# Float32 scores for two attentions, on two halves of TensorE's rows

## The chip, the cores and the metric

The kernel runs on one core of one Trainium2 chip. The metric is the device time of one execution in microseconds (us); lower is better. All data are in float32 outside the chip. TensorE takes its operands either as plain float32 or as float32r, a rounded form that the program makes with a cast.

## The reference

A bidirectional encoder of two layers over 1024 tokens of width 1024. In each layer a mixing block joins three groups of features, and a gated feed-forward block follows:

```python
for l in range(DEPTH):
    h = _rmsnorm(x, g_pre_mix[l])
    zf, zq, zk, zv, zm = jnp.split(h @ w_in[l], splits, axis=-1)
    y_f = _fourier_mix(zf, w_fourier[l])
    q = _rope(zq.reshape(b, s, 8, 64), positions)
    k = _rope(zk.reshape(b, s, 2, 64), positions)
    y_a = _window_attn(q, k, zv.reshape(b, s, 2, 64), sink[l])
    km, vm = jnp.split(_rmsnorm(mem, g_mem[l]) @ w_mem_kv[l], 2, axis=-1)
    y_m = _memory_attn(zm.reshape(b, s, 4, 64), km, vm)   # km, vm: 256 rows, 4 heads
    y = jnp.concatenate([_rmsnorm(y_f, ...), _rmsnorm(y_a, ...), _rmsnorm(y_m, ...)], axis=-1) @ w_out[l]
    x = x + _rmsnorm(y, g_post_mix[l])
    h = _rmsnorm(x, g_pre_ffn[l])
    gate, up = jnp.split(h @ w_ffn_in[l], 2, axis=-1)
    x = x + _rmsnorm((jax.nn.silu(gate) * up) @ w_ffn_out[l], g_post_ffn[l])
```

The window attention has 8 query heads of 64 channels in two groups of four; each group shares one key and value head. A block of 128 queries sees the keys of its own block and of its two neighbours, so 256 keys at the edges and 384 elsewhere, and the softmax has one extra "sink" term for each head. The memory attention has 4 heads of 64 channels over 256 memory rows, and no mask.

## The kernel before

**Precision.** Most products run in float32r. To keep accuracy, an operand is split in two float32r parts: `hi` is a cast by ScalarE (line 176) and `lo` the difference, by VectorE or GpSimd (line 177). A product of split operands is then several float32r matmuls that add up in PSUM (`Acc`, line 187). A few products are plain float32, which TensorE carries out as two instructions each.

**Order of the work.** One instruction stream for each engine; a scheduler orders it from a timeline of its own, with the order of the source as priority, so matmuls of neighbouring streams are interleaved. `weave` mixes lists of units. In each layer the stages run in this order: the Fourier input and the projection of keys, values and memory queries (`kvz`), woven with the Fourier group; the projection of queries (`q`), woven with the memory attention (`mem_units`); the first window group (`att_units(0)`), woven with the output projection of the Fourier and memory groups (`fm_units`, tile `mo`); the second window group (`att_units(1)`) with the output projection of the window group (`out`), the residual and the preparation of the feed-forward blocks (`hb`). The two feed-forward products take the rest of a layer.

**Stacks.** A head has 64 channels, half of the array's 128 rows. The scores use all rows by stacking: `q_stacks` puts the cast of a head's queries on its own 64 partitions and the difference on the other 64, one such tile for each head of a pair (line 435 casts on ScalarE, line 438 subtractions on VectorE). It serves the window queries (`q_turn`, 128 x 512 at a time) and the memory queries (`kvz_turn`, tile `zT`). `dup_stacks` writes the keys likewise, the cast on both halves (lines 424 and 425) and the difference on both halves (428 and 429); it serves the window keys (`kvz_turn`, tile `kT`) and the memory keys (`Memory.load`, from a DMA). The lines 424 to 438 in the profile are these two helpers.

**Scores.** For each head, two float32r matmuls add up in one PSUM bank: the stacked queries against the keys' cast, and against the keys' difference. In the window attention (line 788, tile `sc`) they are 256 or 384 wide and each head has a PSUM tile of its own from the tag `sc` (two tiles). One VectorE instruction adds the mask and takes the maximum (line 789); then ScalarE does the exponential (801) and GpSimd the division (812). In the memory attention (line 901, tile `ms`) a unit is one head with half of the tokens, in two PSUM tiles of 2 x 256 columns; VectorE takes the maxima (903), ScalarE the exponentials with their sums (906), GpSimd the division (912).

**Values.** TensorE transposes the probabilities (825 and 922, tiles `pT` and `mpT`) and they are copied out of PSUM. The first window group splits them (176, 177) and multiplies them by a stack of the values' cast and difference, 512 columns for four heads, twice (840); `fold` then adds the two halves of the result (861 to 863). The second window group copies them unsplit (830) and runs plain float32 (833): heads 0 and 2 on one half of the array's columns, 1 and 3 on the other, 256 columns each; `values_32` adds the values' two parts together beforehand. The memory values are plain float32 in the same manner (932), 512 columns for a head, its two heads from two units.

**Memory.** All SBUF tiles lie in two arenas, one of float32r and one of float32, at hand-chosen places given in units of 1 KB for each partition. A place can be given over to a tile of the other type (`reflex`, `turned`, table `TURNED`). PSUM has 8 banks, shared out by tags (`PS_BUFS`): `sc`, `pT`, `av` and `pd`, two tiles of one bank each.

## Time and profile before

| what | us |
|---|---|
| median of three timed runs | 2032.31 |
| lowest and highest of them | 2031.08, 2033.2 |
| the profiled execution | 2032.38 |
| its span, first to last instruction | 2030.4 |

The granted TensorE clock has a mean of 0.994 of full speed over the span. The feed-forward products fill about 404 to 1000 us in the first layer and 1403 us to the end in the second; the change's stages lie at about 67 to 383 and 1039 to 1380 us.

How to read the profile: PE is TensorE's matmuls, PEld its weight loads, DVE VectorE, ACT ScalarE, POOL GpSimd. `L788` is line 788 of the kernel before. `sc<-arena_r` names the tile written and those read. In `128*128 128x384 f32` the first two numbers are the rows and columns of the array that are in use and the last two the output; `128*64` is a matmul on half of the columns. A group's row has its count, then busy us and mean ns of one, then idle time of the engine before it and what ended it. Matmuls are pipelined and their shown ends are modelled, so the distance from one start to the next says what one costs, not its shown duration. A float32 matmul other than a transpose stands in the profile as two instructions.

### The profile page before, as it was taken

The page shows a single profiled execution, that of the slowest core. Times are in us where ns is not written, and L with a number is a line of the kernel's source. Part 1 is how long each engine was busy: PE and PEld are TensorE (multiplying, and loading weights), DVE is VectorE, ACT ScalarE, POOL GpSimd, SP SyncE. Part 2 cuts the span into 40 slices and gives each one's busy share as a digit, 9 for nine tenths or more (in the row PEclk, how much of TensorE's full clock was granted, in tenths as well). Part 3 has the DMA queues.
Part 4 walks back from the last instruction along what each step waited for, and adds up shares of the span by engine and source line. Part 5 has one row for each costly group of instructions (what it writes and reads, how often), then busy time and mean ns, then how long its engine had stood idle before and what let it go on. Part 6 is the DMA issues. An engine that isn't in the chain of part 4 may idle for free.

```text
span 2030.4 us, 28325 instructions
## 1 busy us (share of the span) xinstructions
PE 1984.7 (98%) x9587; PEld 1631.2 (80%) x9587; DVE 1492.6 (74%) x2346; ACT 1049.7 (52%) x2204; POOL 684.9 (34%) x811
## 2 busy tenths in 40 slices
PE   8999999999999999999999999999999999999998
PEld 7877878778888888887888778877788888887886
DVE  5566767897877776778876668679786776778766
ACT  6476877643333333554555768686333333346441
POOL 4344445224334333002423644451433433410011
PEclk9999999999999999999999999999999999999999
DMA  6110333434333324879831113244333323269973
GB/s 213 62 58 22 109 104 115 146 109 130 104 109 100 103 88 139 297 266 324 286 142 54 54 58 115 85 144 135 106 118 114 116 82 114 96 209 354 314 265 125
DMA packets 181889, 288.56 MB, mean 142 GB/s; under 512 B 15560, under 2 KB 81648, under 8 KB 181744
## 3 DMA queue, kind: packets, MB, share of 16 engines
q1 hardware_dynamic: 173680, 267.88, 39.7%
q10 hardware_dynamic: 8064, 18.88, 2.4%
q8 instruction: 75, 1.23, 0.2%
q14 instruction: 70, 0.57, 0.1%
HBM read 220.11 MB, written 66.58 MB: 141 GB/s over the span
## 4 chain that ended last, share of the span: by engine, by line
PE 86%; DVE 5%; DMA 3%; ACT 2%; issue 2%; POOL 1%; SPq 0%; DVEq 0%; POOLq 0%; ACTq 0%
PE fo L1330 17%; PE qc L1181 11%; PE qx L1181 11%; PE qy L1181 11%; PE mo L187 8%; PE qz L1181 5%; PE kvp L187 4%; PE qp L187 3%; PE zT L187 2%; PE sc L788 2%; PE pT L825 2%; PE av L833 1%; PE qa L1181 1%; PE mav L932 1%; PE av L840 1%
## 5 line engine op out<-in xcount | busy, mean ns | idle before, releaser
L1330 PE MATMUL fo<-arena_r 128*128 128x512 f32 x1512 | 354.2, 391 | 6.0 <-ACT big L1355 3.8
L1330 PEld LDWEIGHTS fo<-arena_r 128*128 128x128 f32 x1512 | 283.6, 188 | 65.6 <-ACT big L1355 4.6
L176 ACT CAST arena_r<-arena_f 128x512 fp32r<-128x512 f32 (+2 forms) x344 | 185.9, 571 | 179.5 <-DMA arena_f<-actd 66.6
L1181 PE MATMUL qc<-arena_r,flex 128*128 128x512 f32 x912 | 220.2, 390 | 0.0
L177 DVE TENSOR_TENSOR arena_r<-arena_f,arena_r 128x512 fp32r<-128x512 f32 x262 | 182.0, 727 | 46.9 <-ACT arena_r L176 39.0
L1171 ACT CAST flex<-arena_f 128x512 fp32r<-128x512 f32 x148 | 91.9, 621 | 235.0 <-PE qy L1181 73.3
L1181 PEld LDWEIGHTS qc<-arena_r,flex 128*128 128x128 f32 x912 | 171.2, 188 | 37.0
L1181 PE MATMUL qy<-arena_r,flex 128*128 128x512 f32 x576 | 139.9, 390 | 2.3 <-ACT flex L1171 2.3
L1171 ACT CAST arena_r<-arena_f 128x512 fp32r<-128x512 f32 x92 | 57.1, 621 | 159.1 <-DVE arena_f L1168 63.6
L1172 DVE TENSOR_TENSOR flex<-arena_f,flex 128x512 fp32r<-128x512 f32 x148 | 110.9, 750 | 28.4 <-ACT flex L1171 28.2
L1181 PEld LDWEIGHTS qy<-arena_r,flex 128*128 128x128 f32 x576 | 107.9, 188 | 25.3 <-ACT flex L1171 2.7
L1215 POOL TENSOR_TENSOR arena_f<-arena_f 128x512 f32<-128x512 f32 x36 | 47.3, 1315 | 237.5 <-ACT arena_f L1186 237.5
L1181 PE MATMUL qx<-arena_r 128*128 128x512 f32 x360 | 119.5, 389 | 0.0
L1181 PE MATMUL qy<-arena_r 128*128 128x512 f32 x480 | 116.7, 390 | 0.0
L1172 DVE TENSOR_TENSOR arena_r<-arena_f,arena_r 128x512 fp32r<-128x512 f32 x92 | 68.2, 742 | 63.2 <-ACT arena_r L1171 62.8
L1181 PE MATMUL qz<-arena_r,flex 128*128 128x512 f32 x320 | 106.8, 395 | 0.0
L1181 PEld LDWEIGHTS qy<-arena_r 128*128 128x128 f32 x480 | 90.3, 188 | 18.9 <-ACT arena_r L1171 0.2
L1168 DVE TENSOR_TENSOR arena_f<-arena_f 128x512 f32<-128x512 f32 x90 | 98.1, 1098 | 5.5 <-DMA arena_f<-in_w_ffn_in 3.9
L1222 POOL TENSOR_TENSOR arena_f<-arena_f 128x512 f32<-128x512 f32 x36 | 60.0, 1667 | 120.2 <-DVE arena_f L1221 120.2
L187 PE MATMUL mo<-big,arena_r 128*128 128x512 f32 x384 | 100.2, 399 | 0.3 <-ACT arena_f L1031 0.2
L1181 PE MATMUL qx<-flex,flex 128*128 128x512 f32 x304 | 100.1, 390 | 0.0
L1242 POOL TENSOR_TENSOR arena_f<-arena_f,flex 128x512 f32<-128x512 f32 x32 | 51.8, 1619 | 139.5 <-ACT flex L1233 83.7
(315 smaller groups left out, 4659.8 us busy)
## 6 DMA issues: line engine op xcount, KB each, us to landing
arena_f<-in_w_ffn_out SPq DMA_DIRECT2D x264, 256.0 KB, 4.7
actd<-arena_f SPq DMA_DIRECT2D x154, 256.0 KB, 2.5
arena_f<-actd SPq DMA_DIRECT2D x154, 256.0 KB, 4.4
arena_f<-in_w_ffn_in SPq DMA_DIRECT2D x46, 512.0 KB, 3.7
big<-in_w_ffn_in SPq DMA_DIRECT2D x40, 512.0 KB, 4.5
arena_f<-in_w_in SPq DMA_DIRECT2D x40, 256.0 KB, 2.9
arena_f<-in_x SPq DMA_DIRECT2D x16, 512.0 KB, 4.3
arena_f<-in_w_out SPq DMA_DIRECT2D x32, 256.0 KB, 2.7
```

The source lines that it names most:

```text
L176: nc.scalar.copy(hi, src)
L177: return (lo_eng or nc.vector).tensor_tensor(out=lo, in0=src, in1=f32(hi), op=ALU.subtract)
L187: mm(self.dst, a, b, start=self.i == 0, stop=self.i == self.n - 1)
L788: mm(pt, lhs, self.kst[g][i][:, k0 * P : k1 * P], start=i == 0, stop=i == 1)
L1168: nc.vector.tensor_tensor(out=s, in0=x, in1=y, op=op)
L1171: self.cast = nc.scalar.copy(w[:, 0], s)
L1172: nc.vector.tensor_tensor(out=w[:, 1], in0=s, in1=f32(w[:, 0]), op=ALU.subtract)
L1181: mm(pt, a, b, start=start and n == 0, stop=n == 11, skip_group_check=not start)
L1215: G(out=self.u2, in0=self.u2, in1=self.p1, op=ALU.add)
L1222: G(out=self.p5, in0=self.p1, in1=self.p5, op=ALU.add)
L1242: (G if i % 2 else V).tensor_tensor(out=a[i], in0=c, in1=g[i], op=ALU.mult)
L1330: mm(pt, ab[:, 0, x, sl], ab[:, 1, y], start=new and first and j == 0, stop=last and j == 2, skip_group_check=not new)
```

## The change

The scores of both attentions become plain float32. Queries, keys and memory queries are copied unsplit; the two heads of a pair lie on partitions 0 to 63 and 64 to 127 and their products are issued one behind the other, each on its 64 rows of the array, into the two banks of one PSUM tile with the new tag `s2` (one tile). A memory unit becomes a pair of heads with a quarter of the tokens. The first window group's values take the second's form, with the evacuating copies in turn on VectorE and ScalarE. `dup_stacks`, `q_stacks`, `fold` and `values_32` go. Places in the arenas move, and some PSUM tags are exchanged.

```diff
-TURNED = {32: 8, 56: 8, 112: 8, 120: 4}
+TURNED = {16: 8, 32: 8, 56: 8, 64: 8, 72: 8, 80: 8, 96: 8, 104: 8, 112: 8, 120: 4}
-PS_BUFS = {"sc": 2, "pT": 2, "av": 2, "pd": 2}
+PS_BUFS = {"sc": 2, "pT": 2, "av": 2, "pd": 2, "s2": 1}
...
         def load(self):
-            raw = at(32, 2, NMEM)
-            nc.sync.dma_start(raw, kvd[self.l, :, 0:512].rearrange("p (i c) -> p i c", i=2))
+            self.k = at(32, 2, NMEM)
+            nc.sync.dma_start(self.k, kvd[self.l, :, 0:512].rearrange("p (i c) -> p i c", i=2))
...
-            km = shaped(reflex(F32R), (2, 2, 2, NMEM))
-            self.km = [km[:, i] for i in range(2)]
-            for ci in range(2):
-                dup_stacks([(self.km[ci][:, j, 0], self.km[ci][:, j, 1]) for j in range(2)], raw[:, ci])
...
             def products(r):
-                pt = ps([256], "yfp", "sc")
+                pt = ps([256], "yfp", "av")
...
         def kvz(self, t):
-            split(vst[:, :, 0, :], vst[:, :, 1, :], r[:, P : 2 * P].rearrange("p (g d) -> p g d", g=2), nc.gpsimd)
+            nc.gpsimd.tensor_copy(self.v32[:, :, t, :], r[:, P : 2 * P].rearrange("p (g d) -> p g d", g=2))
...
         def kvz_turn(self, t):
-            q_stacks([self.zst[half][j][:, :, c * P : c * P + P] for j in range(2)], zt)
+            nc.scalar.copy(self.zf[:, half, :, c * P : c * P + P], zt)
...
-                dup_stacks([(self.kst[g][0][:, sl], self.kst[g][1][:, sl]) for g in range(2)], ktf)
+                for g, copy in enumerate((nc.scalar.copy, nc.vector.tensor_copy)):
+                    for o in range(2):
+                        copy(self.kf[64 * o : 64 * o + 64, g, sl], ktf[64 * g : 64 * g + 64])
...
         def q_turn(self, t):
-            q_stacks([self.qst[half][j][:, :, c * P : c * P + P] for j in range(2)], qt)
+            nc.scalar.copy(self.qf[half][:, :, c * P : c * P + P], qt)
...
         def att_scores(self, g, n):
-            for h in range(4):
-                pt = ps([W], "sc", "sc")
-                lhs = self.qst[half][h % 2][:, 2 * g + h // 2, c * P : c * P + P]
-                for i in range(2):
-                    mm(pt, lhs, self.kst[g][i][:, k0 * P : k1 * P], start=i == 0, stop=i == 1)
-                nc.vector.tensor_tensor_reduce(
...
+            for hp in range(2):
+                pt = ps([2, 512], "sc", "s2")
+                pts = [pt[:, s, :W] for s in range(2)]
+                for s in range(2):
+                    r = slice(64 * s, 64 * s + 64)
+                    mm(pts[s], self.qf[half][r, 2 * g + hp, c * P : c * P + P], self.kf[r, g, k0 * P : k1 * P], start=True, stop=True)
+                for s in range(2):
+                    nc.vector.tensor_tensor_reduce(
...
         def att_values(self, g, n, es_, dst):
-                pp = phs(2, 512, dt=F32R)
-                ph, pl = pp[:, 0], pp[:, 1]
-                split(ph, pl, pT.rearrange("p h q -> p (h q)"))
-                lhs = self.vst[(k0 + j) // 4][:, (k0 + j) % 4, g].rearrange("p a d -> p (a d)")
-                for i, p_ in enumerate((ph, pl)):
-                    mm(av, lhs, p_, start=j == 0 and i == 0, stop=j == nk - 1 and i == 1)
+                pf = self.pfs[self.pfi % 4]
+                self.pfi += 1
+                (nc.vector.tensor_copy if (self.pfi % 2 and not g) else nc.scalar.copy)(pf, pT.rearrange("p (k s) q -> p s k q", s=2))
+                for s in range(2):
+                    rhs = pf[:, s].rearrange("p k q -> p (k q)")
+                    mm(av[64 * s : 64 * s + 64, 0 : 2 * P], self.v32[:, g, k0 + j], rhs, start=j == 0, stop=j == nk - 1)
+            nc.scalar.copy(dst, av[:, 0 : 2 * P].rearrange("p (k q) -> p k q", k=2))
...
+        def mem_scores(self, half, pr, b):
...
+            pt = ps([2, 2, NMEM], "ms", "s2")
+            pts = [pt[:, s] for s in range(2)]
+            for j in range(2):
+                c = 2 * b + j
+                for s in range(2):
+                    r = slice(64 * s, 64 * s + 64)
+                    mm(pts[s][:, j], self.zf[r, half, pr, c * P : c * P + P], self.mem.k[r, pr], start=True, stop=True)
+            for s in range(2):
+                nc.vector.tensor_reduce(out=nmx[:, 2 * s : 2 * s + 2], in_=pts[s], axis=AX.X, op=ALU.max, negate=True)
...
         def mem_turn(self, e):
-                pf = mps(512)
-                nc.scalar.copy(pf, pT.rearrange("p h q -> p (h q)"))
+                pf = mps(2, 256)
+                nc.scalar.copy(pf, pT.rearrange("p s j q -> p s (j q)"))
...
-        def mem_values(self, pr, half, pfs):
-            av = ps([512], "mav", "av")
+        def mem_values(self, half, pr, b, pfs):
+            av = ps([256], "mav", "av")
...
-                    mm(av[64 * s : 64 * s + 64], self.mem.v[:, mt, 2 * pr + s], pfs[s][mt], start=mt == 0, stop=mt == 1)
+                    mm(av[64 * s : 64 * s + 64], self.mem.v[:, mt, 2 * pr + s], pfs[mt][:, s], start=mt == 0, stop=mt == 1)
...
-        HB = {1: (64, 72), 2: (80, 88), 5: (16, 24), 6: (96, None), 3: (0, 8), 7: (32, 40), 4: (104, None)}
+        HB = {1: (64, 104), 2: (80, 72), 5: (16, 24), 6: (96, None), 3: (0, 8), 7: (32, 40), 4: (88, None)}
...
-            pt = ps([512], "qa", "sc")
+            pt = ps([512], "qa", "s2")
...
-                self.c11 = ps([512], "qc", "pT")
+                self.c11 = ps([512], "qc", "sc")
...
-                self.x = ps([512], "qx", "sc")
+                self.x = ps([512], "qx", "pT")
```

More of the change, by code (lines that the diff above doesn't have):

```diff
@@ L716, in kvz @@
             if c == 0:
-                self.vst[half] = at(96 + 4 * half, 4, 2, 2, HD, dt=F32R)
-                z = at(104 + 8 * half, 2, 2, 512, dt=F32R)
-                self.zst[half] = [z[:, i] for i in range(2)]
                 if half == 0:
-                    kst = at(80, 2, 2, S, dt=F32R)
-                    self.kst = [[kst[:, i, j] for j in range(2)] for i in range(2)]
+                    self.v32 = turned(96, 2, 2, NT, HD)[:, 0]
+                    self.zf = turned(104, 2, 2, 512)
+                    self.kf = turned(80, 2, S)
             pt = ps([512], "kvp")
@@ L772, in q_turn @@
             if c == 0:
-                self.qst[half] = [at((64, 0)[half] + 8 * i, 4, 512, dt=F32R) for i in range(2)]
-            q_stacks([self.qst[half][j][:, :, c * P : c * P + P] for j in range(2)], qt)
+                self.qf[half] = turned((64, 72)[half], 4, 512)
+            nc.scalar.copy(self.qf[half][:, :, c * P : c * P + P], qt)
         def att_scores(self, g, n):
@@ L825, in att_values @@
                     nc.tensor.transpose(pT[:, h, :], es_[h // 2][:, h % 2, j * P : j * P + P], ident)
-                if g:
-                    pf = self.pfs[self.pfi % 4]
-                    self.pfi += 1
-                    nc.scalar.copy(pf, pT.rearrange("p (k s) q -> p s k q", s=2))
-                    for s in range(2):
-                        rhs = pf[:, s].rearrange("p k q -> p (k q)")
-                        mm(av[64 * s : 64 * s + 64, 0 : 2 * P], self.v32[:, k0 + j], rhs, start=j == 0, stop=j == nk - 1)
-                    continue
@@ L846, in values_32 @@
-        def values_32(self):
-            self.v32 = at(4, NT, HD)
-            for half in range(2):
-                v = self.vst[half][:, :, 1]
-                nc.gpsimd.tensor_tensor(out=self.v32[:, 4 * half : 4 * half + 4], in0=f32(v[:, :, 0]), in1=f32(v[:, :, 1]), op=ALU.add)
-            pf = turned(112, 4, 2, 2, P)
-            self.pfs, self.pfi = [pf[:, i] for i in range(4)], 0
-        def fold(self, av, dst):
-            cut = lambda ap: ap.rearrange("p (h s q) -> p s h q", s=2, q=P)
-            avh, avl = cut(av[0:64]), cut(av[64:128])
-            d = [dst[64 * s : 64 * s + 64] for s in range(2)]
-            for s in range(2):
-                nc.scalar.copy(d[s], avl[:, s])
-            for s in range(2):
-                nc.vector.tensor_tensor(out=d[s], in0=avh[:, s], in1=d[s], op=ALU.add)
+                pf = self.pfs[self.pfi % 4]
@@ new lines, in att_values, with att_begin @@
+                self.pfi += 1
[4 more added lines that the diff above has]
+            nc.scalar.copy(dst, av[:, 0 : 2 * P].rearrange("p (k q) -> p k q", k=2))
+        def att_begin(self, g):
+            pf = turned((16, 112)[g], 4, 2, 2, P)
+            self.pfs, self.pfi = [pf[:, i] for i in range(4)], 0
+            if g:
+                v = at(4, NT, HD)
+                nc.gpsimd.tensor_copy(v, self.v32[:, 1])
+                self.v32 = v[:, None].to_broadcast([P, 2, NT, HD])
+                reflex(F32R, 16)
+                reflex(F32R, 96)
@@ L910, in mem_scores @@
             nc.vector.reciprocal(rden, den)
-            for b in range(4):
-                nc.gpsimd.tensor_scalar(
-                    out=e[b // 2][:, b % 2], in0=e[b // 2][:, b % 2], scalar1=rden[:, b : b + 1], scalar2=1.0, op0=ALU.mult, op1=ALU.mult
-                )
+            for i in range(4):
+                ei = e[i // 2][:, i % 2]
+                nc.gpsimd.tensor_scalar(out=ei, in0=ei, scalar1=rden[:, i : i + 1], scalar2=1.0, op0=ALU.mult, op1=ALU.mult)
             return e
@@ L942, in unit @@
                     st[i] = self.mem_scores(*todo[i])
[L943 to L945 removed]
+                if i >= 2:
+                    if i == 2:
                         ym = at(24, 2, 2, 512)
                         self.ym = [ym[:, i] for i in range(2)]
[L948 removed]
+                    self.mem_values(*todo[i - 2], pp.pop(i - 2))
                 if 1 <= i <= n:
@@ L1455, in tile_encoder @@
                 uq.load_part(0, at(44, 2, 4, P))
-                reflex(F32R, 112)
+                for k in (72, 80, 112):
+                    reflex(F32R, k)
                 gq.step(1)
```

67 lines of the change are left out of this document (18 added, 49 removed).

## Prediction

> **What bounds the kernel now.** I read the page first, then busy time by stage, the engine's own waits, the groups of matmuls by shape, and last the timeline of TensorE around the places that change. The page, engines and the chain that ended last:
>
> ```profile
> PE 1984.7 (98%) x9587; PEld 1631.2 (80%) x9587; DVE 1492.6 (74%) x2346; ACT 1049.7 (52%) x2204; POOL 684.9 (34%) x811
> ...
> PE 86%; DVE 5%; DMA 3%; ACT 2%; issue 2%; POOL 1%; SPq 0%; DVEq 0%; POOLq 0%; ACTq 0%
> ```
>
> The columns of the next view are stretch, length, then busy us (instructions) of PE, PEld, DVE, ACT and POOL. The stretches of the first layer are those of the memory attention, of the first window group, and of the second.
>
> ```profile
> 138.00:204.00 66.00, 63.90 (x331) 48.99 (x330) 45.50 (x75) 40.80 (x114) 30.32 (x51) 0.97 0.06 19
> 204.00:290.00 86.00, 83.52 (x449) 69.44 (x449) 65.44 (x196) 67.61 (x182) 37.93 (x63) 1.00 0.35 117
> 290.00:383.00 93.00, 91.17 (x531) 72.17 (x530) 64.81 (x134) 66.11 (x164) 45.66 (x77) 0.98 0.36 122
> ```
>
> The reader is to see that TensorE is the bound in each of the three stages (97%, 97% and 98% busy), and that VectorE and ScalarE, which the change relieves, stand at 62 to 79%. Their work counts only where TensorE waited for it. Those waits, of TensorE alone, us in total, times, longest:
>
> ```profile
> PE av L840 <- DVE flex L863: 2.0, 2, 1.3
> ...
> PE qp L187 <- DVE big L407: 1.7, 1, 1.7
> ...
> PE ms L901 <- ACT flex L425: 1.3, 1, 1.3
> ...
> PE ssp L988 <- DVE arena_r L438: 1.1, 2, 0.8
> PE ms L901 <- DVE flex L438: 0.8, 1, 0.8
> ```
>
> These five hang on the splits that go (L425 the keys' casts, L438 subtractions for q, z and keys, L863 the fold) or stand behind them in VectorE's queue (L407, a weight split amid the key splits). Together 6.9 us: nearly all the waiting that the change can take away. So the forecast is a sum over TensorE's work.
>
> **What a matmul costs now.** The groups (line, shape, count | busy us, mean ns; a float32 product shows as two instructions):
>
> ```profile
> L788 PE MATMUL sc<-arena_r 128*128 128x384 f32 x192 | 49.0, 355 | 0.1
> L788 PE MATMUL sc<-arena_r 128*128 128x256 f32 x64 | 12.7, 298 | 0.5 <-ACT arena_f L906 0.3 <-DVE rmax L789 0.2
> L840 PE MATMUL av<-arena_r 128*128 128x512 f32 x88 | 31.0, 420 | 2.2 <-DVE flex L863 2.0 <-DVE arena_r L177 0.2
> L833 PE MATMUL av<-flex,arena_f 128*64 128x256 f32 x176 | 26.3, 398 | 0.0
> L932 PE MATMUL mav<-arena_f 128*64 128x512 f32 x64 | 23.4, 612 | 0.0
> L901 PE MATMUL ms<-flex,arena_r 128*128 128x256 f32 x64 | 10.4, 289 | 2.1 <-ACT flex L425 1.3 <-DVE flex L438 0.8
> L901 PE MATMUL ms<-flex,flex 128*128 128x256 f32 x64 | 10.2, 286 | 0.0
> ```
>
> The mean durations overlap, so they don't add up. What one costs is read from the starts of consecutive timeline rows (start, length, line, shape, count):
>
> ```profile
> 160.05 0.64 PE L901 MATMUL ms<-flex,arena_r 128*128 128x256 f32 x4
> 160.52 0.40 PE L187 MATMUL qp<-big,flex 128*128 128x512 f32 x1
> ...
> 280.86 1.07 PE L840 MATMUL av<-arena_r 128*128 128x512 f32 x4
> 281.77 0.87 PE L788 MATMUL sc<-arena_r 128*128 128x384 f32 x4
> 282.48 0.86 PE L187 MATMUL mo<-big,arena_r 128*128 128x512 f32 x3
> ...
> 293.82 0.65 PE L833 MATMUL av<-flex,arena_f 128*64 128x256 f32 x4
> 294.40 0.61 PE L988 MATMUL ssp<-const,arena_f 128*128 128x2 f32 x4
> ...
> 298.34 0.88 PE L788 MATMUL sc<-arena_r 128*128 128x384 f32 x4
> 299.14 0.65 PE L833 MATMUL av<-flex,arena_f 128*64 128x256 f32 x4
> ...
> 308.07 1.52 PE L833 MATMUL av<-flex,arena_f 128*64 128x256 f32 x12
> 309.52 0.96 PE L187 MATMUL mo<-flex,arena_r 128*128 128x512 f32 x3
> 310.32 0.40 PE L187 MATMUL mo<-arena_r 128*128 128x512 f32 x1
> ```
>
> Split (float32r) products, four each: 160.52 - 160.05 = 0.47 us at 256 columns, 282.48 - 281.77 = 0.71 at 384, 281.77 - 280.86 = 0.91 at 512 (0.23 each). A float32 pair on two halves of the array's columns, 256 wide, is four instructions: 0.58 alone (294.40 - 293.82), and three pairs 1.45 (309.52 - 308.07). So each further pair costs (1.45 - 0.58)/2 = **0.435**, and a run of pairs has 0.145 of its own. The rest of its price falls on its neighbours: four score products ahead of a run took 0.80 (299.14 - 298.34) instead of 0.71, 0.09 more; behind it three 512-wide products took 0.80 (310.32 - 309.52) instead of 3 x 0.23, 0.11 more. A run thus costs 0.145 + 0.09, and up to 0.11 where a split product follows: 0.24 to 0.35 beside its streaming; I take **0.30**, the middle. The streaming itself, 0.435 for two heads at 256 columns, is what split products need too (0.47).
>
> **The change part by part.**
>
> *Window scores.* Per two heads, four split products give way to one float32 pair on two halves of the rows. There are 64 such pairs (192/4 = 48 wide, 64/4 = 16 narrow). No pair on row halves stands in the trace; the nearest row is the pair on column halves. Streaming scales to 0.435 x 1.5 = 0.65 at 384. Wide: 0.65 + 0.30 - 0.71 = +0.24, x48 = 11.5; narrow: 0.435 + 0.30 - 0.47 = +0.265, x16 = 4.2. Together **+15.7**. The bounds are a run that costs nothing extra (64 x 0.30 = 19.2 less) and halves that run one after the other (rival 2).
>
> *Memory scores.* 128 split products in 16 units; a unit's eight took 0.94. Now two pairs in one run: 0.87 + 0.30 = 1.17, so +0.23 x16 = **+3.7**.
>
> That entering a row tile costs anything has one row, a transpose on 8 rows of the array:
>
> ```profile
> 25.64 0.62 PE L187 MATMUL zT<-arena_r 128*128 128x512 f32 x2
> 26.20 0.23 PE L262 MATMUL posT<-const,flex 8*128 8x8 f32 x1
> 26.35 1.20 PE L187 MATMUL zT<-arena_r 128*128 128x512 f32 x4
> ```
>
> The two products ahead took 0.56 instead of 0.46, 0.10 more, as ahead of a column run, and the tiny transpose held the engine 0.15. So I take the column price for rows. The Trainium skill, TensorEngine Tiling (Array Packing), Tiling Modes, Key Properties, says that changing the tiling mode drains TensorE; that speaks against the change, and by it the sum is the forecast's, without it rival 1's. The Trainium skill, TensorE: Matmul & The Clock Gate, Part 3, says that tiles on different rows run together with starts some 4 ns apart; no run here shows it for rows, and by it rival 2 falls away.
>
> *First group's values.* 88 split products of 0.23 (20.3) become 44 pairs of 0.435 (19.1) as in the second group, whose 176 instructions (44 pairs, from 293.82 to 1368.9) came in 33 runs: 19.1 + 33 x 0.30 = 29.0, **+8.7**; bounds 22 and 44 runs, +5.4 and +12.
>
> *Memory values.* Now some heads' products run alone:
>
> ```profile
> 205.06 1.07 PE L932 MATMUL mav<-arena_f 128*64 128x512 f32 x2
> 206.06 0.50 PE L788 MATMUL sc<-arena_r 128*128 128x256 f32 x2
> ```
>
> One product, 1.00 us, with half the columns empty. After, both heads of a pair come from one evacuated tile, so 32 pairs of 256 columns: 32 x 0.435 + 16 to 32 runs x 0.30 = 18.7 to 23.5, against 23.4 busy now. I take **-3**.
>
> *Neighbouring runs.* Score runs that fall next to another float32 run share one change of mode. Guess: 20 of 80 save 0.2 each, **-4**; bounds 0 and -10.
>
> *Splits that go.* Two rows of VectorE:
>
> ```profile
> L177 DVE TENSOR_TENSOR arena_r<-pT,arena_r 128x512 fp32r<-128x512 f32 x44 | 29.4, 687 | 1.3 <-ACT arena_r L176 0.8
> ...
> L438 DVE TENSOR_TENSOR arena_r<-qT,arena_r 64x512 fp32r<-64x512 f32 x32 | 22.0, 689 | 9.9 <-ACT arena_r L435 9.4
> ```
>
> These alone are 51.4 us of VectorE; half of the 44 come back as copies of about the same length (15). All of it lies beside TensorE except the 6.9 us of waits above: **-7**, bounds 0 and -10. The keys now come straight from their load, a wait that ended behind eight casts and eight subtractions; behind it the load itself is next, some microseconds earlier. The moved buffers, the value copy on GpSimd (a copy for a subtraction of the same size) and the exchanged PSUM tags add no DMA and no queue entry: nothing, hidden under TensorE's 97%; without that cover about one copy, 0.7 each.
>
> *New wait.* Scores now have one tile of two banks where they had two tiles. Its prices:
>
> ```profile
> L789 DVE CUSTOM_DVE_ANT_0 arena_f<-sc,const 128x384 f32<-128x384 f32 x96 | 51.2, 552 | 24.6 <-PE sc L788 14.7 <-PE pT L825 5.6 <-POOL arena_r L177 3.0
> L903 DVE TENSOR_REDUCE nmx<-ms 128x2 f32<-128x512 f32 x32 | 21.3, 687 | 7.9 <-PE ms L901 7.5
> L906 ACT ACTIVATE arena_f<-ms,nmx 128x256 f32<-128x256 f32 x64 | 29.7, 473 | 26.8 <-DVE nmx L903 26.7
> L906 ACT ACTIVATION_READ_ACCUMULATOR arena_f<-ms,nmx 128x1 f32 x64 | 13.0, 202 | 0.0
> ```
>
> A window pair holds the tile 0.95 + 2 x 0.55, some 2.1 us, twice per block of 86/8 = 10.8 us. A memory unit holds it 1.2 + 0.7 + 4 x 0.68 = 4.6 of 66/8 = 8.3 us. Behind a waiting score matmul in TensorE's queue stand q projections, output products and transposes, and for those wait the ScalarE copies; but the tile is free about half the time, so I take 0 (bounds 0 and +12, rival 3).
>
> Sum: 15.7 + 3.7 + 8.7 - 3 - 4 - 7 = **+14**. The profiled execution took 2032.38 us, its span 2030.4 and 2.0 around it; the median of the three shown is 2032.31, the same. Forecast 2032.4 + 14 = 2046.
>
> **The rivals.**
>
> 1. *Row halves need no change of mode* (other side: faster). Then 80 runs lose 0.30 each, and the sharing of 4 goes: 14 - 24 + 4 = -6, **2026**. For: no pair on rows is in the trace, and all columns stay in use. Against: the row transpose's 0.10 and 0.15. It decides below about 0.10 us a run.
> 2. *The halves run one after the other*: the streaming comes twice, 48 x 0.65 + 16 x 0.435 + 32 x 0.435 = +52, **2098**. Against: column pairs do run together (0.58 for four instructions of 256).
> 3. *The single two-bank tile becomes a wait*: at the ends of the memory stage and of a window stage there is little else to issue; two units at two stages in two layers, 1.5 us each, +12, **2058**. For: a memory unit's hold is over half of its interval. Against: the present score waits are 0.5 us in all.
> 4. *More hides than thought*: score runs mostly join value runs (-10 for -4), 22 value runs (-3) and 10 us of waits (-3): +2, **2034**, which is no change.
>
> **How the numbers follow.** Forecast 0.48 (own range 2037 to 2056), rival 1 0.20, rival 2 0.09, rival 3 0.12, rival 4 0.11. About 0.2% (4 us) is what a measurement here can tell from no change. Rival 1 gives faster 0.14 and same 0.06; rival 4 splits into same 0.08 and faster 0.03; the rest is slower: 0.17, 0.14, 0.69. The range holds the forecast, rivals 1, 3 and 4: 2024 to 2064; it leaves out rival 2 and the tails.
>
> **What would show it.** Right: float32 score rows on 64 rows in two instructions each, partners starting a few ns apart; 0.9 to 1.0 us from a lone wide pair to the next start; L425, L438 and L863 gone from TensorE's waits; TensorE's busy time in the memory and window stages up by about 14 in all. Wrong: partners hundreds of ns apart (rival 2), a lone pair at 0.65 to 0.75 (rival 1), waits of score matmuls for L789 or L906 of microseconds (rival 3).

## The result and the profile after

| kernel | median of the timings, us | lowest and highest | profiled execution | its span |
|---|---|---|---|---|
| before | 2031.12 (6) | 2030.23, 2033.2 | 2032.38 | 2030.4 |
| after | 2077.5 (6) | 2073.34, 2079.84 | 2076.18 | 2074.4 |

The ratio is 1.0224, with a 95% interval of 1.021 to 1.0237: the change makes the kernel slower by 46 us. The forecast was 14 us slower, in a range up to 2064. The direction came true, the size did not: it is over three times the forecast, and outside the range.

The page of the changed kernel, engines and the chain that ended last:

```profile
PE 2016.1 (97%) x9739; PEld 1593.6 (77%) x9739; DVE 1423.9 (69%) x2212; ACT 1002.6 (48%) x2094; POOL 697.1 (34%) x809
...
PE 82%; DVE 6%; DMA 4%; issue 3%; ACT 2%; POOL 2%; DVEq 0%; POOLq 0%; ACTq 0%; SPq 0%
```

VectorE lost 69 us of work (1492.6 before) and ScalarE 47, as the diff promises, and TensorE gained 31.4. The span has grown by more than that. **Idle time of TensorE is span less busy time**: 2030.4 - 1984.7 = 45.7 before, 2074.4 - 2016.1 = 58.3 now. So the 44.0 us of span are 31.4 of TensorE's work and 12.6 of waiting. This subtraction is used for every kernel below.

A part of the work is clock. Counted over the trace, TensorE's granted clock stood at 0.50 for 27.0 us before and for 33.7 now (in both some 2 us of the last stretch lie behind the span). At half the clock at most half of the time is lost, so up to (33.7 - 27.0)/2 = 3.4 of the 31.4 is that, and 28 or a little more is matmuls.

The three stretches of the first layer that the prediction showed, at the same times and in the same columns (the stages now lie a few microseconds later):

```profile
138.00:204.00 66.00, 66.00 (x372) 49.20 (x371) 29.07 (x51) 34.18 (x98) 31.92 (x56) 1.00 0.08 25
204.00:290.00 86.00, 83.63 (x450) 51.77 (x451) 45.78 (x146) 50.00 (x139) 34.33 (x57) 1.00 0.30 101
290.00:383.00 93.00, 92.89 (x515) 63.49 (x514) 57.37 (x136) 65.54 (x170) 44.43 (x76) 1.00 0.29 98
```

VectorE fell from 65.44 to 45.78 us in the first group's stage, and TensorE stands at 97% to 100% as before. Relief of an engine that did not set the pace can buy no more there than the waits tied to it.

The groups of matmuls that replaced those of the prediction (line, shape, count | busy us, mean ns | idle before, releaser). L763 are the window scores, L807 the values, L857 and L887 the memory attention's scores and values:

```profile
L763 PE MATMUL sc<-flex,flex 64*128 64x384 f32 x192 | 44.9, 535 | 0.0
L807 PE MATMUL av<-flex,arena_f 128*64 128x256 f32 x176 | 28.3, 404 | 0.0
L807 PE MATMUL av<-flex,flex 128*64 128x256 f32 x176 | 27.4, 401 | 1.2 <-DVE flex L804 1.1
L857 PE MATMUL ms<-arena_f,flex 64*128 64x256 f32 x128 | 19.1, 405 | 1.6 <-ACT arena_f L862 1.6
L887 PE MATMUL mav<-arena_f 128*64 128x256 f32 x96 | 18.0, 413 | 2.7 <-ACT arena_f L879 2.7
L763 PE MATMUL sc<-flex,flex 64*128 64x256 f32 x64 | 12.5, 446 | 0.1
```

`64*128` says that these matmuls use 64 rows of the array. The four instructions of one wide pair start at 214.440, 214.447, 214.868 and 214.875 us: partners stand 7 ns apart, so the halves do run together. By busy time the wide scores have even become cheaper (44.9 for 49.0). That reading misleads, as the timeline of TensorE shows (start, length, line, shape, count):

```profile
237.37 1.63 PE L187 MATMUL mo<-big,arena_r 128*128 128x512 f32 x6
238.84 0.60 PE L801 MATMUL pT<-const,arena_f 128*128 128x128 f32 x4
239.37 0.92 PE L763 MATMUL sc<-flex,flex 64*128 64x384 f32 x4
240.21 1.69 PE L187 MATMUL mo<-big,arena_r 128*128 128x512 f32 x6
241.74 0.60 PE L801 MATMUL pT<-const,arena_f 128*128 128x128 f32 x4
242.09 1.63 PE L187 MATMUL mo<-big,arena_r 128*128 128x512 f32 x6
243.65 1.08 PE L807 MATMUL av<-flex,flex 128*64 128x256 f32 x8
244.66 0.61 PE L942 MATMUL ssp<-const,arena_f 128*128 128x2 f32 x4
```

Take differences of starts. Six output products take 1.47 when transposes follow (238.84 - 237.37), 1.56 when a run of values follows (243.65 - 242.09): **0.09 ahead** of a run. Behind the score pair the same six take 1.53 (241.74 - 240.21): **0.06 behind**. The pair itself holds 0.84 (240.21 - 239.37), of which 0.65 is streaming: **0.19 of its own**. Together 0.34 for a run on half the rows. The run of two value pairs took 1.01 (244.66 - 243.65), 0.14 beside 2 x 0.435; with the same neighbours' parts 0.29 for a run on half the columns. What falls on the neighbours is in no row of the scores' own line.

The neighbours' parts depend on what the neighbours are. Four transposes take 0.35 in front of output products (242.09 - 241.74) and 0.53 in front of the score pair (239.37 - 238.84): 0.18 ahead of a run where transposes stand, twice what the products lose, and half of the window scores' runs stand behind transposes. The 0.06 behind is one row; over the six such places of the trace that no wait and no half clock disturbs, products of 512 columns behind a row run and in front of transposes lose 0.02 in the median.

The Trainium skill, TensorEngine Tiling (Array Packing), Tiling Modes, Key Properties, says that changing the tiling mode drains TensorE; these 0.09 to 0.18, 0.19 and 0.06 agree with it.

TensorE's waits, total us, times, longest:

```profile
PE fo L1284 <- ACT big L1309: 8.0, 2, 4.7
...
PE mav L887 <- ACT arena_f L879: 2.7, 3, 1.5
PE qz L1135 <- ACT arena_r L1125: 2.6, 2, 1.3
...
PE kT L712 <- POOL arena_f L681: 2.4, 2, 1.8
...
PE ms L857 <- ACT arena_f L862: 1.6, 1, 1.6
...
PE mo L187 <- ACT arena_r L176: 1.3, 1, 1.3
...
PE av L807 <- DVE flex L804: 1.1, 1, 1.1
PE mo L187 <- ACT arena_f L985: 1.1, 2, 0.9
...
PE mpT L877 <- POOL arena_f L869: 0.6, 1, 0.6
```

The five waits that the forecast took away (6.9 us) are gone, though for the weight split a wait of 1.0 for its cast (L406) stands where L407 had 1.7. Others stand in their place: those shown, apart from L1309's and L1125's, lie in the attention's part of a layer and come to 10.8 us. None is a wait of the window scores. L1309, a copy in the feed-forward block, rose from 3.8 to 8.0. In the kernel before it was

```profile
PE fo L1330 <- ACT big L1355: 3.8, 2, 2.9
```

The instructions there are the same as before; what the change touches in that block are places in the arenas and the PSUM tags of the product ahead (`qa`, `qc`, `qx`).

### The profile page after: what moved, and what is told of

Read it like the earlier page. It is cut to its first block, busy times and chain, and to the rows that moved or that the text cites. A ratio compares the mean times of both kernels' runs of the same rounds, so it can differ in the third digit from the quotient of the medians.

```text
span 2074.4 us, 28265 instructions
## 1 busy us (share of the span) xinstructions
PE 2016.1 (97%) x9739; PEld 1593.6 (77%) x9739; DVE 1423.9 (69%) x2212; ACT 1002.6 (48%) x2094; POOL 697.1 (34%) x809
## 4 chain that ended last, share of the span: by engine, by line
PE 82%; DVE 6%; DMA 4%; issue 3%; ACT 2%; POOL 2%; DVEq 0%; POOLq 0%; ACTq 0%; SPq 0%
PE fo L1284 15%; PE qy L1135 11%; PE qx L1135 11%; PE qc L1135 10%; PE mo L187 8%; PE qz L1135 5%; PE qp L187 4%; PE kvp L187 3%; PE sc L763 2%; PE av L807 2%; PE zT L187 2%; PE pT L801 2%; DMA arena_f<-actd 2%; DMA arena_f<-in_w_ffn_out 1%; PE mav L887 1%
## 5 line engine op out<-in xcount | busy, mean ns | idle before, releaser
L1284 PE MATMUL fo<-flex 128*128 128x512 f32 x1176 | 285.0, 395 | 6.5 <-ACT big L1309 3.3
L1284 PEld LDWEIGHTS fo<-flex 128*128 128x128 f32 x1176 | 223.7, 191 | 53.9 <-ACT big L1309 3.8
L1135 PE MATMUL qc<-flex,flex 128*128 128x512 f32 x912 | 221.0, 391 | 0.0
L1125 ACT CAST flex<-arena_f 128x512 fp32r<-128x512 f32 x148 | 91.5, 621 | 233.8 <-PE qy L1135 64.8
L176 ACT CAST flex<-arena_f 128x512 fp32r<-128x512 f32 (+1 forms) x228 | 130.0, 606 | 150.6 <-DMA arena_f<-actd 66.8
L1135 PEld LDWEIGHTS qc<-flex,flex 128*128 128x128 f32 x912 | 171.2, 188 | 36.8
L177 DVE TENSOR_TENSOR flex<-arena_f,flex 128x512 fp32r<-128x512 f32 x204 | 145.8, 739 | 62.0 <-ACT flex L176 52.1
L1284 PE MATMUL fo<-arena_r 128*128 128x512 f32 x672 | 165.2, 392 | 4.7 <-ACT big L1309 4.7
L1284 PEld LDWEIGHTS fo<-arena_r 128*128 128x128 f32 x672 | 126.6, 189 | 31.4 <-ACT big L1309 5.1
L1125 ACT CAST arena_r<-arena_f 128x512 fp32r<-128x512 f32 x92 | 56.9, 621 | 161.1 <-DVE arena_f L1122 67.4
L1126 DVE TENSOR_TENSOR flex<-arena_f,flex 128x512 fp32r<-128x512 f32 x148 | 113.7, 768 | 25.1 <-ACT flex L1125 24.9
L1135 PE MATMUL qx<-flex,arena_r 128*128 128x512 f32 x384 | 125.8, 390 | 0.0
L1126 DVE TENSOR_TENSOR arena_r<-arena_f,arena_r 128x512 fp32r<-128x512 f32 x92 | 68.0, 741 | 63.8 <-ACT arena_r L1125 63.8
```

Of the source, the lines that this page charges most:

```text
L176: nc.scalar.copy(hi, src)
L177: return (lo_eng or nc.vector).tensor_tensor(out=lo, in0=src, in1=f32(hi), op=ALU.subtract)
L1125: self.cast = nc.scalar.copy(w[:, 0], s)
L1126: nc.vector.tensor_tensor(out=w[:, 1], in0=s, in1=f32(w[:, 0]), op=ALU.subtract)
L1135: mm(pt, a, b, start=start and n == 0, stop=n == 11, skip_group_check=not start)
L1284: mm(pt, ab[:, 0, x, sl], ab[:, 1, y], start=new and first and j == 0, stop=last and j == 2, skip_group_check=not new)
```

## Experiments

The expectations name their theories by letters, as their own texts say them. A is throughout that the added time is matmul work at a price for each run, so that every part of the change brings its own share.

### Each half of the change alone

`values_only` is the kernel before with only the first group's values in the new form. `scores_only` is the changed kernel with that group's values split as before.

```diff
 values_only, against before
-                pp = phs(2, 512, dt=F32R)
...
-                for i, p_ in enumerate((ph, pl)):
-                    mm(av, lhs, p_, start=j == 0 and i == 0, stop=j == nk - 1 and i == 1)
...
+                for s in range(2):
+                    rhs = pf[:, s].rearrange("p k q -> p (k q)")
+                    mm(av[64 * s : 64 * s + 64, 0 : 2 * P], self.v32[:, g, k0 + j], rhs, start=j == 0, stop=j == nk - 1)
 scores_only, against after: the same lines the other way round, for g == 0
```

> The kernel before with one part of the change alone: the first window group's values in plain float32, in the second group's form. Theory A (each run of float32 matmuls on part of the array costs 0.33 us beside its streaming): 44 pairs x 0.435 + about 40 runs x 0.33 = 32 us against 20 for the split products, less 2 us of waits for the fold: +10, about 2041. Theory B (the single two-bank score tile makes TensorE wait): no such tile here, so 2031. Theory C (the order of the whole kernel is redrawn and waits turn up anywhere, the feed-forward stages included): anything from 2026 to 2046, with the difference outside the first window group's stage.

> The changed kernel with the first window group's values split as before; the float32 scores of both attentions stay. Theory A: 64 window runs (+20 against the split scores), 16 memory runs (+5), memory values about even, less 5 us of waits for key and query splits: +20, about 2051. Theory B: all of the loss stays, about 2077. Theory C: between 2045 and 2070, with waits in stages that the scores don't touch.

`values_only` took 2038.73 (ratio 1.0047, 1.0027 to 1.0067). The engines' row of its page, span 2036.7:

```profile
PE 1993.1 (98%) x9675; PEld 1624.9 (80%) x9675; DVE 1470.6 (72%) x2292; ACT 1028.2 (50%) x2150; POOL 691.2 (34%) x809
```

8.4 us more of work (up to 2.2 of it clock, 31.4 us at 0.50) and an idle time of 43.6, 2.1 less: theory A holds for this half. `scores_only` took 2083.8 (1.0258, 1.0241 to 1.0276), 6 us **more** than the whole change. Its row, span 2081.7:

```profile
PE 2013.3 (97%) x9651; PEld 1602.3 (77%) x9651; DVE 1443.6 (69%) x2266; ACT 1025.6 (49%) x2148; POOL 701.2 (34%) x811
```

28.6 of work and an idle time of 68.4, 22.7 above the kernel before. Theory A had put this kernel at 2051 and misses by 33. So the waits come with the scores and what they bring with them (the tile, the tags, the places), not with the values; and beside the new scores the new values, a loss of some 8 by themselves, save 6, by 10 us less idle time.

### Is it the one tile of two banks?

`two_tiles` is the changed kernel with the pair's scores in two tiles of one bank, and the PSUM tags as before. `before_one_tile` is the kernel before, split products and all, with its scores in one tile of two banks; the tags that the change exchanged are exchanged there too.

```diff
 two_tiles, against after
-                pt = ps([2, 512], "sc", "s2")
-                pts = [pt[:, s, :W] for s in range(2)]
+                pts = [ps([W], "sc", "sc") for s in range(2)]
...
-            pt = ps([2, 2, NMEM], "ms", "s2")
-            pts = [pt[:, s] for s in range(2)]
+            pts = [ps([2, NMEM], "ms", "sc") for s in range(2)]
 before_one_tile, against before
-                pt = ps([W], "sc", "sc")
+                if h % 2 == 0:
+                    two = ps([2, 512], "sc", "s2")
+                pt = two[:, h % 2, :W]
...
+            two = ps([2, 2, NMEM], "ms", "s2")
-                pt = ps([2, NMEM], "ms", "sc")
+                pt = two[:, b]
```

> The changed kernel with the scores of a pair in two tiles of one bank each, as before the change, and all PSUM tags as before; the float32 matmuls and their pairs stay. TensorE's waits (of over 0.15 us) sum to 44.6 us in the changed kernel and 32.1 before. Theory A (the price of the runs): the runs stay, so the loss in matmul time of some 28 us stays, and the time is 2072 to 2080. Theory B (the single two-bank tile makes the additional 12 us of waits): they go, 2065. Theory C (order redrawn): waits anywhere between 35 and 55 us.

> The kernel before with only its PSUM tiles changed: split scores as before, but those of two heads (window) or of a unit's two halves (memory) in one tile of two banks, and the tags of the changed kernel. Theory A: no more runs, so no more than a few us, 2031 to 2035. Theory B: 8 to 12 us of waits for the tile, 2040. Theory C: 2026 to 2036 with waits in other stages.

`before_one_tile` took 2135.92 (1.0529, 1.0509 to 1.0548): the one tile, with the tags that were exchanged for it, costs the kernel before 105 us. Its waits of TensorE:

```profile
PE sc L790 <- DVE rmax L791: 21.6, 35, 1.2
PE mpT L925 <- POOL arena_f L915: 6.6, 5, 2.7
PE av L842 <- ACT arena_r L176: 5.0, 3, 2.8
```

Here the score matmul itself waits 35 times for the VectorE instruction that empties the tile. Idle time is 2132.7 - 2034.8 = 97.9, 52 above the kernel before. The clock was at 0.50 for 71.6 us, up to another 22. Some 28 more are TensorE's busy time on the same matmuls; by differences of starts they stand at the scores, the values and the transposes around them, and why is not shown. The tile and the tags were not tried apart. In the changed kernel the same tile does far less harm. There VectorE has 69 us less to do, and would empty it sooner; that this is the reason fits, and no run varied it alone. If so, the relief of VectorE mostly pays for a cost that the change itself brings.

`two_tiles` took 2092.65 (1.0301, 1.0286 to 1.0315), slower still. Its row, span 2091.7:

```profile
PE 2042.6 (98%) x9739; PEld 1612.8 (77%) x9739; DVE 1419.5 (68%) x2212; ACT 1002.7 (48%) x2094; POOL 689.8 (33%) x809
```

The idle time went from 58.3 to 49.1, most of the way to the 45.7 of before. The waits of the memory scores and values (1.6 and 2.7 above) aren't in its list any more. But the work rose by 26.5, up to 8.7 of it clock (51.0 us at 0.50), and TensorE's timeline says where the rest comes from:

```profile
216.37 0.91 PE L762 MATMUL sc<-flex,flex 64*128 64x384 f32 x2
217.21 0.44 PE L800 MATMUL pT<-const,arena_f 128*128 128x128 f32 x2
217.58 0.91 PE L762 MATMUL sc<-flex,flex 64*128 64x384 f32 x2
218.42 1.66 PE L187 MATMUL mo<-big,arena_r 128*128 128x512 f32 x6
```

With a tile of its own each half goes when its own bank is free, and something comes between. A lone half takes 0.84 (217.21 - 216.37), as long as a whole pair. Only 27 times did two halves start together, against 62 of 64 in the changed kernel. So the tile of two banks keeps the pair together and goes with the waits; no run here had the one without the other, and a second such tile, which would need two banks more, was not tried. The fall of idle time is weaker proof than `before_one_tile`, since a slower TensorE also leaves the others more time.

### Memory attention split again

`mem_split` is the changed kernel with the memory attention as before, except that its scores stay in the one tile of two banks: one head with half the tokens, eight split products.

```diff
-            pt = ps([2, 2, NMEM], "ms", "s2")
-            pts = [pt[:, s] for s in range(2)]
-                    mm(pts[s][:, j], self.zf[r, half, pr, c * P : c * P + P], self.mem.k[r, pr], start=True, stop=True)
+            pt2 = ps([2, 2, NMEM], "ms", "s2")
+            for b in range(2):
+                pt = pt2[:, b]
+                        mm(pt[:, j], lhs, self.mem.km[h // 2][:, h % 2, i], start=i == 0, stop=i == 1)
```

> The changed kernel with the memory attention as before (split scores of one head and half of the tokens in a unit, stacked keys and queries), though its scores take the one two-bank tile. Theory A: 16 score runs fewer (-5), some 12 memory value runs fewer but some products alone again (0): about 2072. Theory B: the tile is still single, held as long by a unit: no change, 2077. Theory C: within 6 us of 2077 either way.

It took 2099.77 (1.035, 1.0332 to 1.0367), 22 above the changed kernel, where theory A said 2072. Fewer runs (166 for 192) gave no gain: TensorE's work is 2029.4 - 2016.1 = 13.3 above the changed kernel's, and the idle time is 2093.0 - 2029.4 = 63.6. The memory transposes wait:

```profile
PE mpT L905 <- POOL arena_f L895: 4.6, 7, 1.6
```

In the changed kernel that wait is 0.6, in the row of L877 above. As in `before_one_tile`, the split form under the one tile is the worse mix here; where the 13.3 of work come from was not tried.

### The price of a run

`runs_joined` is the changed kernel with all value products of a block issued one behind the other, after the last of their copies, and the memory values likewise. `merged_g0` moves the first group's products one unit later instead.

```diff
 runs_joined, against after
-            av = ps([512], "av", "av")
+            pfs = []
...
+                pfs.append(pf)
+            av = ps([512], "av", "av")
+            for j in reversed(range(nk)):
...
-            for mt in range(2):
+            for mt in (1, 0):
 merged_g0, against after
+            late = SKEW + (g == 0)
+                if g == 0 and i >= late:
+                    products(i - late)
```

> The changed kernel with the value products of a block issued last tile first, in both window groups and in the memory attention: the product that waits longest opens the sum, so the others can't run ahead and all of a block stand in one run. Same arithmetic, same number of matmuls. By the order of TensorE's instructions some 57 value runs in place of 108. Theory A (a price of 0.33 us for each run of float32 matmuls on part of the array): 50 x 0.33 = 16 less, about 2061. Theory B (waits on the single two-bank score tile): no change, 2077 or more. Theory C (a redrawn order costs, wherever it falls): within 6 us of 2077, whatever the number of runs.

> The changed kernel, with the first window group's value products of a block issued one unit later, when all of its two or three transposed tiles have been copied, so that they can stand together in one run. Same arithmetic. Theory A: some 40 runs become 16 to 20, 20 to 24 fewer at 0.33: -7, about 2070, and the profile shows runs of 8 and 12 instructions. Theory B: no change, 2077. Theory C: within 6 us of 2077 either way, whatever the number of runs.

`merged_g0` took 2083.01 (1.026, 1.0245 to 1.0275). The scheduler still issued each product as it became ready: the values' runs were 78, one fewer than without the edit. So it says nothing on the price. `runs_joined` took 2068.03 (1.0175, 1.0149 to 1.0201), 9.5 below the changed kernel where 16 was expected. Its runs fell from 192 to 139 (values 79 to 33, memory values 29 to 20). Its groups of values, where the changed kernel had 28.3 and 27.4:

```profile
L810 PE MATMUL av<-flex,arena_f 128*64 128x256 f32 x176 | 23.5, 401 | 0.0
L810 PE MATMUL av<-flex,flex 128*64 128x256 f32 x176 | 22.7, 389 | 2.1 <-ACT flex L804 2.1
```

TensorE's work fell by 2016.1 - 2009.6 = 6.5, and the clock was at 0.50 for 45.0 us instead of 33.7, which can hide up to 5.6 more: up to 12 us for 53 runs, 0.23 each, and 0.12 without the clock. Counting each matmul to the start of the next, with the waits and half of the time at 0.50 left out, gives 11.2, or 0.21. At 0.30 it should have been 16. The price of a run is real; here it is smaller than the timeline gives it.

### The same joints in the kernel before

`before_joined` takes the joined second group and paired memory units into the kernel before, `g1_joined` the first alone, `mem_joined` the second alone. `tiles_only` is the kernel before with its arenas cut into the change's smaller tiles (all but one, 16 KB at 80) and nothing else.

```diff
 g1_joined, against before
-                    for s in range(2):
-                        rhs = pf[:, s].rearrange("p k q -> p (k q)")
-                        mm(av[64 * s : 64 * s + 64, 0 : 2 * P], self.v32[:, k0 + j], rhs, start=j == 0, stop=j == nk - 1)
+                    pfs.append(pf)
...
+                for j in reversed(range(nk)):
 mem_joined, against before
-        def mem_scores(self, h, half):
+        def mem_scores(self, half, pr, b):
...
-            todo = [(h, half) for half in range(2) for h in range(4)]
+            todo = [(half, pr, b) for half in range(2) for pr in range(2) for b in range(2)]
 tiles_only, against before
-TURNED = {32: 8, 56: 8, 112: 8, 120: 4}
+TURNED = {16: 8, 32: 8, 56: 8, 64: 8, 72: 8, 80: 16, 96: 8, 104: 8, 112: 8, 120: 4}
```

> The kernel before (split scores and first group) with the changed kernel's memory units (two heads and a quarter of the tokens), so that both heads' value products are ready together, and with the value products of the memory and of the second window group issued last tile first. Theory A: memory values 17 runs and 19.7 us of streaming become 16 runs and 13.8, second group 33 runs become 16: 6 + 6 = 12 less, about 2019. Theory C: within 6 us of 2031 either way.

> The kernel before with the second window group's value products issued last tile first, so that 33 runs become 16; nothing else. Theory A: 17 x 0.33 = 6 us less TensorE work; 2026 if no wait takes its place, 2031 if the waits that grew with it in the kernel with both joins belong to this part.

> The kernel before with the memory units of the changed kernel (two heads, a quarter of the tokens, scores still split) and their value products joined; the second window group as before. Theory A: 6 us less TensorE work; 2026 if no wait takes its place, 2031 if the waits that grew belong to this part.

> The kernel before with nothing changed but that the arena of split data is cut into more separate tiles, at the places where the changed kernel cuts it; every instruction is as before. Theory A and B: no change, 2031. Theory C (the finer tiles alone redraw order and waits): 2036 to 2044, with waits in the start and in the feed-forward stages.

| kernel | median, us | ratio (interval) | work against before | idle, us |
|---|---|---|---|---|
| g1_joined | 2033.73 | 1.0018 (1.0008 to 1.0029) | -4.6 | 49.4 |
| mem_joined | 2029.85 | 1.0004 (0.9992 to 1.0016) | -6.5 | 49.6 |
| before_joined | 2030.85 | 0.9991 (0.9978 to 1.0004) | -11.0 | 52.2 |
| tiles_only | 2030.69 | 0.9994 (0.9978 to 1.001) | -1.2 | 44.6 |

The cut of the arenas costs nothing; that theory falls. The other three show something that the forecast had left out. Work taken off TensorE, 4.6, 6.5 and 11.0, does come off in the page's busy time (17 runs fewer in `g1_joined` at 0.30 are 5.1), and more than half of it comes back as idle time (3.7, 3.9 and 6.5 above 45.7). The medians move by 0.2% at most. A kernel at 98% busy is still not one where each microsecond of the busiest engine counts in full.

### The waits in the feed-forward block

`evac_dve` is the changed kernel with the copy that L1284 waits for moved from ScalarE to VectorE.

```diff
-                    nc.scalar.copy(c11[p], pt)
+                    nc.vector.tensor_copy(c11[p], pt)
```

> The changed kernel with one of the two copies that empty each PSUM tile after the first product of the feed-forward output moved from ScalarE to VectorE; TensorE waits 8.0 us for these copies in the changed kernel (3.8 before). If these waits are part of the loss: 5 to 8 less, 2070. If they only move to the next step: 2077.

It took 2084.5 (1.0255, 1.023 to 1.028), 7 above the changed kernel. The wait moved and did not go:

```profile
PE fo L1284 <- DVE big L1309: 10.4, 2, 5.4
```

Most of the 7 lies elsewhere, in a stretch far ahead of the edit. Stretches of the changed kernel; the last three columns are the granted clock, the DMA share and GB/s:

```profile
205.00:210.00 5.00, 3.80 (x20) 1.84 (x20) 2.25 (x12) 1.24 (x3) 1.84 (x4) 1.00 0.33 105
210.00:215.00 5.00, 5.00 (x30) 2.88 (x28) 2.50 (x11) 4.00 (x14) 1.75 (x4) 1.00 0.02 7
215.00:220.00 5.00, 5.00 (x31) 3.82 (x28) 2.79 (x9) 4.01 (x14) 3.13 (x6) 1.00 0.27 101
```

and of `evac_dve`:

```profile
205.00:210.00 5.00, 3.79 (x20) 1.88 (x20) 2.34 (x12) 1.24 (x3) 1.84 (x4) 1.00 0.32 105
210.00:215.00 5.00, 5.00 (x20) 2.50 (x16) 1.68 (x8) 3.22 (x12) 0.55 (x1) 0.50 0.01 3
215.00:220.00 5.00, 5.00 (x15) 2.88 (x14) 1.20 (x4) 1.40 (x3) 3.11 (x6) 0.50 0.14 52
```

Both kernels issue the same matmuls in the same order here, and in both TensorE waits 1.2 us between 205 and 210. Behind that, one goes on at full clock, the other at half for 13.7 us. Half of 13.7 is 6.9. The stretch is seen in the one profiled execution, but the mean granted clock was 0.989 to 0.991 in all four runs of `evac_dve` and 0.991 to 0.996 in the six of the changed kernel, which fits. By the stages the first layer's attention is 6.2 longer than in the changed kernel, and no other part more than 1.2; the medians differ by 7.0.

## Why the prediction was right or wrong

| step | forecast | in the profile |
|---|---|---|
| matmuls (work, clock taken out) | +21 | +28 |
| waits of TensorE | -7 | +12.6 |
| clock | not reckoned | up to +3.4 |
| span | +14 | +44.0 |

**What bounds the kernel.** Right that relief of VectorE and ScalarE buys only the waits tied to it. Too simple in taking TensorE's work one for one: `before_joined` gives more than half of a saving back.

**Rivals 1 and 2.** Both fall. Partners start 7 ns apart and a whole pair costs what a lone half does (0.84), so the halves don't run one after the other. A row run has its price: 0.84 to the next start where rival 1 asked for 0.65 to 0.75. The forecast named 0.9 to 1.0 there; only 0.19 of the price lies before the next start, the rest on the neighbours.

**Window and memory scores.** The mechanism was right, and the price taken from column runs a little low: 0.34 for 0.30 by the timeline above, more where transposes stand ahead. Two of the 64 pairs came apart, at 0.65 and 0.435 of streaming and a run each. So the window scores are (0.65 + 0.34 - 0.71) x 48 + (0.435 + 0.34 - 0.47) x 16 + 1.8 = +20 for +15.7. The memory scores, 32 pairs in 18 runs, are 13.9 + 6.1 - 15.0 = +5 for +3.7.

**First group's values.** The price held (0.29), the count didn't. Values came in 79 runs where the second group had 33 before: 46 more, above even the bound of 44. At 0.30 that is 19.1 + 13.8 - 20.3 = +12.6 for +8.7. `values_only`, at +8.4 of work and 30 more runs, still agrees with the forecast's count; the other runs came apart only beside the new scores.

**Memory values.** 29 runs, near the upper end of 16 to 32: 13.9 + 8.7 = 22.6 against 23.4, a gain of 1 and not 3. **Neighbouring runs.** 192 runs have 346 changes of form instead of 384; at the 0.1 that a change costs beside a run, 38 shared ones save some 4. The guess of 4 came out by luck: it had 20 shared changes at 0.2.

These terms add up to +33, the page says +28. The traces place the difference. Count each matmul to the start of the next one, with waits of over 0.15 us and half of the time at 0.50 left out: the two attention parts hold 23.8 us more, and 8.6 more of their work (24 output products, 16 transposes, 8 small sums) now comes after the first feed-forward matmul. That is 32, as the terms say. The start of the kernel holds 4 less, nearly all on matmuls that did not change in number, and waits 4 more. The whole kernel has 29.8 more by this count. By the same count the scores' and values' own lines gained only 6.6 (the split window scores had cost 47.7 and not the 41.6 of the sum: four of 384 columns take 0.79 behind transposes, not 0.71). Output products gained 10.1 and the transposes of the probabilities 10.4. Most of what the runs cost stands in rows that the change left alone.

**Splits that go, and the new wait: the steps that failed.** The waits of L425, L438 and L863 did go. But the forecast let -7 stand for all of TensorE's waiting: it took 0 for the new wait ("the tile is free about half the time, so I take 0") and nothing for the moved buffers and the exchanged PSUM tags ("no DMA and no queue entry: nothing"). The idle time rose by 12.6. Cut at the first starts of `kvp` (attention part), `qc` and `fo` (feed-forward block) in each layer, it lies here:

| part | span before, us | longer now by | idle before | idle now | idle in `two_tiles` | idle in `before_one_tile` |
|---|---|---|---|---|---|---|
| start | 67.3 | 0.7 | 13.2 | 17.4 | 13.6 | 16.5 |
| attention, first layer | 314.7 | 6.3 | 6.4 | 2.5 | 1.2 | 24.7 |
| feed-forward, first layer | 657.1 | 13.9 | 6.4 | 11.3 | 12.7 | 7.7 |
| attention, second layer | 337.7 | 18.0 | 3.8 | 9.8 | 3.4 | 32.3 |
| feed-forward, second layer | 653.6 | 5.2 | 15.9 | 17.3 | 18.2 | 16.7 |

The last row holds the 8.6 to 9.0 us behind the last matmul too (8.7 in `before_one_tile`).

In the two attention parts the idle time went from 10.2 to 12.3, where 6.9 less would have left 3.3. So 9.0 us of new waits stand for the 0 of the sum. In `two_tiles` 4.6 stand there, and in `before_one_tile` 57.0: these waits go with the one tile and its tags. The second layer's attention says so in every kernel: 9.2 to 11.9 us idle in seven with the tag `s2` and 32.3 in the eighth, `before_one_tile`, against 3.0 to 7.0 in the six without. "Free about half the time" put a queue's cost at the mean of its load. Rival 3 had the mechanism and near its size (+12), but looked for it in the wrong row. In the changed kernel the window's score matmuls wait for nothing (0.0 and 0.1 in their groups); the waits stand at memory scores, memory values, transposes and output products. It would fit that the scheduler puts the scores where the tile is free and what depends on them comes late; no run shows that.

The other 10.5 of idle time lie outside the attention, where the forecast had nothing. The 4.2 at the start made it only 0.7 longer, as its busy time fell by 3.5. No scores are computed there, yet the start's idle time is 16.3 to 17.4 in the eight kernels with the tag `s2` and 12.5 to 13.6 in the six without it: it goes with the tile or its tags, and how was not tried.

**Clock.** The forecast had no term for it, although the kernel before had 27 us at half clock in plain sight.

**The feed-forward blocks, and what stays open.** They are 19.1 of the 44 us longer. 8.6 of these are the attention's work that moved there, 6.3 waits, and up to 3.4 clock (13.6 us at 0.50 there, 6.8 before, the last stretch of each left out). Of the waits, 4.2 are the one for L1309. That wait is 7.5 to 10.7 us in the seven kernels with the new scores, `two_tiles` among them, and 2.9 to 4.3 in the seven without them, `before_one_tile`, `values_only` and `tiles_only` among these. So neither the one tile nor the finer tiles bring it, but something that came with the new scores; the moved places of the feed-forward operands (`HB`) are one candidate that no run tried alone. The blocks also grow by 5.6 in `before_joined`, where nothing near them changed. That the scheduler draws the order anew from its own estimates is likely, and was not tried.

None of these kernels beats the kernel before by more than the measurement tells.

## What to carry to other kernels

Plain float32 on part of the array saves casts and subtractions, but each run of it cost TensorE about a third of a microsecond here, about half of it on its neighbours' rows; count the runs, not the matmuls, and join them before counting on a gain. Two halves that must start together need both their banks at one time, so price the lost second buffer by trying that alone in the old kernel. The waits that a change brings can stand far from the lines it edits, so look at idle time as a whole (span less busy), then part by part, before looking for it by name.

## What the runs showed of the hardware

A half of a pair, 384 columns on 64 rows, took 0.84 us alone, and two halves together 0.84 to 0.85. Four transposes took 0.35 us in front of output products and 0.53 in front of a run on half the rows.

The granted clock fell to 0.50 for stretches of 3.4, 6.8, 10.2 and 13.7 us: whole multiples of 3.4, but for the last stretch of each kernel, which runs past its end. With the same matmuls and the same two waits of 0.6 us ahead, one kernel had none of it and another 13.7 us. The Trainium skill, TensorE: Matmul & The Clock Gate, Part 1, names two states of the clock, full and half, decided over free-running windows of about 3.4 us. The lengths and the 0.50 agree. That the place of a wait within such a window decides would fit the two kernels; no run here varied it.
